# Sums of squares by one-column matmuls, taps at the front, and layer 1's memory product behind the mean matmul, in a two-layer decoder kernel

## The chip, the cores and the metric

The kernel runs on one core of a Trainium2 chip. The metric is the device time of one execution in microseconds; before the change the median of three runs is 2445.08 (2444.04 to 2449.28). TensorE is PE in the profile, VectorE DVE, ScalarE ACT, GpSimd POOL, and SP issues the DMAs.

## What is computed

A decoder trunk of two layers on x of 1024 tokens by 1024, with a memory of 256 tokens. The part that the change touches is layer 0's token mixing:

```python
mem_n = rms_norm(mem, mem_norm_g)
for l in range(DEPTH):
    mkv = (mem_n @ w_mem_kv[l]).reshape(B, MEM_LEN, 2, MEM_HEADS, HEAD_DIM)
    mk = rms_norm(mkv[:, :, 0], mem_k_norm_g[l])
    mv = mkv[:, :, 1]
    h = rms_norm(x, norm_mix_g[l])
    # layer 0
    u = h @ a_w_in[i]
    conv_out = conformer_conv(u[..., :2 * CONV_W] + a_b_glu[i], a_dw[i], a_dw_b[i], a_ln_g[i], a_ln_b[i])
    qm = rms_norm(u[..., 2 * CONV_W:].reshape(B, S, MEM_HEADS, HEAD_DIM), mem_q_norm_g[l])
    mix = jnp.concatenate([conv_out, memory_attention(qm, mk, mv)], axis=-1)
    x = x + mix @ w_out[l]
    x = x + squared_relu_mlp(rms_norm(x, norm_mlp_g[l]), w_mlp_in[l], w_mlp_out[l])
```

`conformer_conv` multiplies by a sigmoid gate, runs a causal depthwise convolution of 31 taps over 768 channels, and ends in a layer norm over the 768 channels and a silu. Layer 1 (sparse attention over shared keys and values) is not touched.

## The kernel before

Channels lie on the 128 partitions and tokens along the free axis, in two halves of 512 tokens. A tile is 128x512 in fp32. Each product is three matmuls (high x high, high x low, low x high parts, `mm3`, L80 to L82); `weight` splits a weight tile (ACT L110 the high part, POOL or DVE L111 the low part), and L87/L88 do the same for activations.

A framework with a scheduler puts each engine's instructions into one fixed order, from the order in which the code yields them and from its own model of time. On an engine nothing overtakes: an instruction that waits holds up all that stand behind it.

`layer0` runs layer 0's mixing. Its front, `load(hf)`, brings the eight x tiles of a half in (16 DMAs of 256 KB on SP for both halves) and squares them on ACT; DVE and POOL add the squares into two tiles `facc` (L559). `norm_steps` then makes the RMS norm: `col_stats` sums each column over the partitions by matmuls whose moving operand has one column of ones (L151, four for each part, result `ps_n`), DVE takes the inverse root in three Newton steps (`rsqrt`, L93 to L97) and spreads it over a diagonal (`diag`, L157), and a matmul with ones broadcasts it to all partitions (`ps_r`, L165). DVE multiplies x by it (`h`, L181).

Between the two halves' norms stands layer 0's memory product, `mem_kv`: `product` (L273 to L275, into `ps_mkv`) and `put`, which normalizes the keys by head (`hm`, `hr`, `kn`, split into `khl`) and transposes them by matmuls with the identity (`ps_dk`, L219). Layer 1's memory product is the same code, run later.

Then come six convolution tiles. For tile i of a half the input projection gives `ps_a`, ACT the gate, DVE the gated value `vA` (first half) or `vB` (second half) (L535). `conv(i)` runs 22 of the 31 taps on DVE (L495 the first, L497 the others, into `ca` in PSUM), and nine on ACT and POOL (L500 to L504, `cmore`); L506 adds both, and POOL adds the result to `csum` (L510). The letters of `ORDER` give the sequence in which the code issues these pieces (A and B a tile's projections, M and X the memory queries and attention, F and G the end of the convolution's norm, N and Z the steps of the memory product).

`conv_norm` makes the layer norm of the convolution: `ps_mu` (L634) is the sum over channels of `csum`, DVE subtracts the mean from each tile (L638), ACT squares it (`csq`), POOL and DVE add the squares (L647, L649), `col_stats` and `ps_r` follow as above, DVE scales (L656), and ACT and DVE form the silu (`z`, `t`, L661 to L664). Its eight `act` tiles (six from here and two from the memory attention) go into the output projection, `ps_wo` (L407 to L409).

The taps are loaded after `later()` has opened the pools that follow the front.

Of the kernel before, what the change touches and what calls it, by code (L numbers as in the profile page):

```python
# [89 lines left out]

def rsqrt(nc, r, m, t):

    nc.vector.tensor_scalar(r.bitcast(I32), m.bitcast(I32), -0.5, 1597463007.0, op0=ALU.mult, op1=ALU.add)  # L93
    for _ in range(3):
        nc.vector.tensor_mul(t, r, r)
# [46 lines left out]


def col_stats(k, parts, n, eps, ps=None):

    nc = k.nc
    if ps is None:
        ps = k.psum.tile([P, HF], F32, tag=k.tag, name="ps_n", bufs=k.nps)
    for i, a in enumerate(parts):
        for j in range(4):  # L150
            nc.tensor.matmul(ps[:, j:j + 1], lhsT=a[:, j * P:(j + 1) * P], rhs=k.ones[:, 0:1],  # L151
                             start=(i == 0 and j == 0), stop=(i == len(parts) - 1 and j == 3))
    m, r, t = (k.tmp.tile([P, 4], F32, tag=n_, name=n_, bufs=2) for n_ in ("nm", "nr", "nt"))
    nc.vector.tensor_scalar(m, ps[:, 0:4], 1.0 / n, eps, op0=ALU.mult, op1=ALU.add)
    rsqrt(nc, r, m, t)
    d = k.tmp.tile([P, 4, P], F32, tag="diag", name="diag", bufs=1)
    nc.vector.tensor_mul(d, k.ident[:, None, :].to_broadcast([P, 4, P]), r[:, :, None].to_broadcast([P, 4, P]))  # L157
    return d
# [80 lines left out]

def mem_kv(k, mp, zp, kv0, kv1, kvd, room):  # L240

# [23 lines left out]
    def product(l):  # L265
        pss = [k.psum.tile([P, HF], F32, tag="mm", name="ps_mkv", bufs=4) for _ in range(2)]
        for kt in range(KT):
            at = slice(kt % 2 * 512, kt % 2 * 512 + 512)
            hl = weight(k, k.i["w_mem_kv"][l, kt // 2][:, at], raw=raws[kt // 2][:, at] if l == 0 else None)
            for tt in range(2):  # L270
                ah = mh[kt][:, 0, tt * P:(tt + 1) * P]
                al = mh[kt][:, 1, tt * P:(tt + 1) * P]
                nc.tensor.matmul(pss[tt], lhsT=ah, rhs=hl[:, 0], start=(kt == 0), stop=False)  # L273
                nc.tensor.matmul(pss[tt], lhsT=ah, rhs=hl[:, 1], start=False, stop=False)
                nc.tensor.matmul(pss[tt], lhsT=al, rhs=hl[:, 0], start=False, stop=(kt == KT - 1))  # L275
        k.pe(10400)
# [208 lines left out]
def conv(k, i, v, taps, out, csum, pool, nd):  # L485
# [27 lines left out]
def layer0(k, act, later, finish, dst, kvd, m0d, room, act_b):  # L513

# [5 lines left out]
    with ExitStack() as left:  # L520
# [25 lines left out]
        with tc.tile_pool(name="xfront", bufs=1, side="right") as xp:  # L546

            def load(hf):
                x, acc = [], [xp.tile([P, HF], F32, tag="facc", name="facc", bufs=4) for _ in range(2)]
                for kt in range(KT):  # L550
                    x.append(xp.tile([P, HF], F32, tag="x", name="x", bufs=15))
                    nc.sync.dma_start(x[kt], k.i["x"][hf, :, kt])
                    if kt < 2:
                        nc.scalar.activation(acc[kt], x[kt], AF.Square)
# [4 lines left out]
                    (nc.gpsimd if j else nc.vector).tensor_tensor(acc[j], acc[j], sq, op=ALU.add)  # L559
# [69 lines left out]
def conv_norm(k, mix, cvs, csum, early, order):  # L629
# [3 lines left out]
    ps = k.psum.tile([P, HF], F32, tag=k.tag, name="ps_mu", bufs=k.nps)  # L633
    nc.tensor.matmul(ps, lhsT=k.ones, rhs=csum, start=True, stop=True)  # L634
    acc = csum
    for n, i in enumerate(order):
        c = cvs[i]
        nc.vector.scalar_tensor_tensor(c, ps, -1.0 / 768, c, op0=ALU.mult, op1=ALU.add)  # L638
        if not early:
            sq_add(k, csum, c, n == 0)  # L640
            continue
        t = csum if n == 0 else k.tmp.tile([P, HF], F32, tag="acc" if n == 3 else "a", name="csq", bufs=2)
        if n == 3:
            acc = t
        mark = nc.scalar.activation(t, c, AF.Square)
        if n not in (0, 3):
            (nc.vector if n > 3 else nc.gpsimd).tensor_tensor(acc, acc, t, op=ALU.add)  # L647
    if early:
        nc.vector.tensor_add(csum, csum, acc)  # L649
    d = col_stats(k, [csum], 768, 1e-5)  # L650
    r = col_bcast(k, d)
# [741 lines left out]
```

## Time and profile before

| what | value |
|---|---|
| median of three runs | 2445.08 us |
| lowest, highest | 2444.04, 2449.28 us |
| the profiled execution | 2451.38 us |
| its span | 2449.6 us |
| its mean granted PE clock | 0.988 |

The profile is of one execution, a little longer than the median. Its span counts from the first to the last instruction. A row of its timeline gives the start, how long the instruction lasts, its engine and line, what it writes and reads, and in brackets for how long the engine had been idle and what ended that. PE's rows overlap, since matmuls are pipelined; the distance from one start to the next is the pace.

### The profile page before, as it was taken

What the parts mean: (1) busy time and instruction counts of PE and PEld (TensorE: products, weight loads), DVE (VectorE), ACT (ScalarE), POOL (GpSimd) and SP (SyncE); (2) the same over time, 40 slices, a digit from 0 to 9 for tenths busy, and PEclk for the clock granted to TensorE, in tenths of its full rate; (3) what the DMA queues carried; (4) which work ended last, traced back from release to release, by engine and by line L of the source; (5) the groups of instructions that cost most, each with busy time, mean ns of one, the idle gap of its engine ahead of it and who ended that gap; (6) DMA issues with size and microseconds to landing.
All of it is one profiled execution on the core that took longest, in us unless ns stands there. A gap on an engine that the chain in (4) does not pass through costs nothing.

```text
span 2449.6 us, 36781 instructions
## 1 busy us (share of the span) xinstructions
PE 2362.6 (96%) x12098; PEld 1994.6 (81%) x12098; DVE 1669.2 (68%) x3590; ACT 1293.3 (53%) x2938; POOL 1229.9 (50%) x1060
## 2 busy tenths in 40 slices
PE   5998899999988999999999999999999999999999
PEld 4887687888777988888887888888888887788887
DVE  7897586998668667777436866778787765333333
ACT  5575555333545457777434545666766654333332
POOL 2876544545643256566445324565566542344443
PEclk9999999999999999999999999999999999999999
DMA  5212433323344332322335443322222226233233
GB/s 186 80 55 84 151 97 101 102 92 95 123 128 141 112 115 84 91 79 79 114 103 171 136 130 92 112 64 67 80 80 63 62 67 206 69 95 97 93 96 103
DMA packets 157214, 250.87 MB, mean 102 GB/s; under 512 B 17632, under 2 KB 48992, under 8 KB 156512
## 3 DMA queue, kind: packets, MB, share of 16 engines
q1 hardware_dynamic: 157024, 248.52, 33.0%
q8 instruction: 96, 1.57, 0.3%
q14 instruction: 94, 0.77, 0.1%
HBM read 217.52 MB, written 20.45 MB: 97 GB/s over the span
## 4 chain that ended last, share of the span: by engine, by line
PE 62%; DVE 4%; DMA 3%; issue 2%; ACT 1%; POOL 1%; SPq 0%; ACTq 0%; DVEq 0%; POOLq 0%
PE ps_i L448 7%; PE ps_i L450 7%; PE ps_i L449 7%; PE ps_mo L80 6%; PE ps_mo L82 6%; PE ps_mo L81 6%; PE ps_t L1054 4%; PE ps_s L1010 4%; PE ps_o L1070 2%; PE ps_o L1073 2%; PE ps_tok L688 1%; PE ps_tok L687 1%; PE ps_tok L689 1%; PE ps_wo L409 1%; PE ps_wo L407 1%
## 5 line engine op out<-in xcount | busy, mean ns | idle before, releaser
L111 POOL TENSOR_TENSOR hl<-raw,hl 128x512 fp32r<-128x512 f32 x596 | 778.6, 1317 | 873.8 <-ACT hl L110 830.7
L110 ACT ACTIVATE hl<-raw 128x512 fp32r<-128x512 f32 x648 | 405.1, 630 | 631.6 <-PE ps_i L450 258.1
L470 DVE TENSOR_TENSOR x<-x,ps_mo 128x512 f32<-128x512 f32 x512 | 348.3, 683 | 136.8 <-PE ps_mo L82 133.4
L80 PE MATMUL ps_mo<-hid,hl 128*128 128x512 f32 x1024 | 409.3, 400 | 6.9 <-DVE x L470 6.7
L448 PE MATMUL ps_i<-act,hl 128*128 128x512 f32 x1024 | 407.5, 398 | 8.2 <-DVE x L411 6.9
L450 PE MATMUL ps_i<-act,hl 128*128 128x512 f32 x1024 | 405.7, 396 | 0.0
L449 PE MATMUL ps_i<-act,hl 128*128 128x512 f32 x1024 | 404.0, 395 | 1.2 <-DVE act L417 1.2
L82 PE MATMUL ps_mo<-hid,hl 128*128 128x512 f32 x1024 | 401.2, 392 | 0.0
L81 PE MATMUL ps_mo<-hid,hl 128*128 128x512 f32 x1024 | 400.9, 391 | 0.0
L448 PEld LDWEIGHTS ps_i<-act,hl 128*128 128x128 f32 x1024 | 193.7, 189 | 49.4 <-DVE x L411 7.3
L80 PEld LDWEIGHTS ps_mo<-hid,hl 128*128 128x128 f32 x1024 | 192.3, 188 | 49.5 <-DVE x L470 12.7
L456 DVE SCALAR_TENSOR_TENSOR a<-ps_i,r 128x512 f32<-128x512 f32 x128 | 88.0, 689 | 206.5 <-PE ps_i L450 201.6
L449 PEld LDWEIGHTS ps_i<-act,hl 128*128 128x128 f32 x1024 | 193.6, 189 | 41.8 <-DVE act L417 2.2
L450 PEld LDWEIGHTS ps_i<-act,hl 128*128 128x128 f32 x1024 | 193.5, 189 | 41.9 <-issue 0.5
L82 PEld LDWEIGHTS ps_mo<-hid,hl 128*128 128x128 f32 x1024 | 192.2, 188 | 41.1
L81 PEld LDWEIGHTS ps_mo<-hid,hl 128*128 128x128 f32 x1024 | 192.7, 188 | 37.0 <-issue 0.5
L1021 ACT ACTIVATE prob<-ps_s,small 128x512 f32<-128x512 f32 (+3 forms) x240 | 141.1, 590 | 83.0 <-DVE small L1019 52.7
L1040 POOL TENSOR_TENSOR prob<-prob,small 128x1024 f32<-128x1024 f32 (+3 forms) x120 | 180.0, 1524 | 1.3 <-DVE small L1034 0.8
L1062 DVE TENSOR_TENSOR PT<-ps_t,PT 128x512 fp32r<-128x512 f32 (+1 forms) x220 | 147.0, 671 | 48.2 <-ACT PT L1058 46.9
L1058 ACT ACTIVATE PT<-ps_t 128x512 fp32r<-128x512 f32 (+1 forms) x256 | 142.3, 566 | 60.9 <-PE ps_t L1054 55.0
L1010 PE MATMUL ps_s<-KS,Q 128*128 128x512 f32 (+5 forms) x552 | 143.1, 358 | 0.0
L88 DVE TENSOR_TENSOR hid<-a,hid 128x512 fp32r<-128x512 f32 x128 | 100.6, 787 | 59.0 <-ACT hid L87 58.3
(295 smaller groups left out, 4708.8 us busy)
## 6 DMA issues: line engine op xcount, KB each, us to landing
raw<-in_w_mlp_in_dram SPq DMA_DIRECT2D x256, 256.0 KB, 2.8
raw<-in_w_mlp_out_dram SPq DMA_DIRECT2D x256, 256.0 KB, 2.9
raw<-in_w_out_dram SPq DMA_DIRECT2D x64, 256.0 KB, 3.3
Q<-Q SPq DMA_DIRECT2D x160, 64.0 KB, 2.0
raw<-in_cmp_w_dram SPq DMA_DIRECT2D x32, 256.0 KB, 2.7
raw<-in_a_w_dram SPq DMA_DIRECT2D x24, 256.0 KB, 3.0
raw<-in_b_wq_dram SPq DMA_DIRECT2D x24, 256.0 KB, 2.7
mixd<-ev SPq DMA_DIRECT2D x80, 64.0 KB, 2.1
```

Source lines behind the costliest of these rows:

```text
L80: nc.tensor.matmul(ps, lhsT=lh, rhs=rh, start=(i == 0), stop=False)
L81: nc.tensor.matmul(ps, lhsT=lh, rhs=rl, start=False, stop=False)
L82: nc.tensor.matmul(ps, lhsT=ll, rhs=rh, start=False, stop=(i == n - 1))
L110: nc.scalar.activation(hl[:, 0, :n], raw[:, :n], AF.Copy)
L111: k.last_lo = k.lo_eng.tensor_tensor(hl[:, 1, :n], raw[:, :n], hl[:, 0, :n].bitcast(F32), op=ALU.subtract)
L448: nc.tensor.matmul(p_, lhsT=wh, rhs=h[kt][:, 0], start=kt == 0, stop=False)
L449: nc.tensor.matmul(p_, lhsT=wh, rhs=h[kt][:, 1], start=False, stop=False)
L450: nc.tensor.matmul(p_, lhsT=wl, rhs=h[kt][:, 0], start=False, stop=kt == KT - 1)
L470: nc.vector.tensor_add(x[o], x[o], ps)
L1010: nc.tensor.matmul(o_, lhsT=lhs, rhs=rhs, start=(n_ == 0), stop=(n_ == len(mms) - 1))
L1040: nc.gpsimd.tensor_tensor(t, t, sc[:, :, None].to_broadcast([P, 2, t.shape[-1]]), op=ALU.mult)
L1062: nc.vector.tensor_sub(PT[:, 1, :m], Tv[:, :m], PT[:, 0, :m].bitcast(F32))
```

## The change

1. `col_sums`: the one-column matmuls take the squares tile by tile. At the front each x tile's square goes straight into four of them (32 for a half, 8 before); the adds into `facc` go, and four square tiles `fsq` are kept in place of two. In the first half's conv norm (`early`) the six squares give 24 matmuls where four stood; the adds L647 and L649 go. The second half's conv norm keeps its adds.
2. The last convolution tile is no longer added to `csum`; a second matmul adds it into `ps_mu`.
3. `rsqrt` multiplies in another order, and in `col_stats` the values m, t and the last r stand in columns of `ps_n`'s PSUM bank.
4. The taps are loaded behind the first half's x tiles, into a pool that lives through the kernel.
5. Layer 1's memory product is issued after the mean matmul, and its `put` comes behind the last step of the conv norm (`Z1` at the end of `ORDER`).

```diff
-ORDER = "B0A1M0X0B1A2A3B2A4B3A5B4B5F0M1Z0G0N1"
+ORDER = "B0A1M0X0B1A2A3B2A4B3A5B4B5F0M1Z0G0N1Z1"
...
-    for _ in range(3):
-        nc.vector.tensor_mul(t, r, r)
-        nc.vector.scalar_tensor_tensor(t, t, -0.5, m, op0=ALU.mult, op1=ALU.mult)
-        nc.vector.scalar_tensor_tensor(r, t, 1.5, r, op0=ALU.add, op1=ALU.mult)
+    for i in range(3):
+        nc.vector.tensor_mul(t, r, m)
+        nc.vector.scalar_tensor_tensor(t, t, -0.5, r, op0=ALU.mult, op1=ALU.mult)
+        nc.vector.scalar_tensor_tensor(r if last is None or i < 2 else last, t, 1.5, r, op0=ALU.add, op1=ALU.mult)
...
+def col_sums(k, ps, a, first, last):
+    for j in range(4):
+        k.nc.tensor.matmul(ps[:, j:j + 1], lhsT=a[:, j * P:(j + 1) * P], rhs=k.ones[:, 0:1], start=(first and j == 0),
+                           stop=(last and j == 3))
...
-    m, r, t = (k.tmp.tile([P, 4], F32, tag=n_, name=n_, bufs=2) for n_ in ("nm", "nr", "nt"))
+    r = k.tmp.tile([P, 4], F32, tag="nr", name="nr", bufs=2)
+    m, t, last = (ps[:, 4 * i:4 * i + 4] for i in range(1, 4))
...
+                if l == 1:
+                    es.enter_context(k.tc.issue_after(behind().ins))
...
     pss = product(1)
+    yield
     KS, V = kv1()
...
-    else:
+    elif i < 5:
         nc.gpsimd.tensor_tensor(csum, csum, out, op=ALU.add)
...
-                    if kt < 2:
-                        nc.scalar.activation(acc[kt], x[kt], AF.Square)
-                        continue
-                    sq = xp.tile([P, HF], F32, tag="fsq", name="fsq", bufs=2)
+                    sq = xp.tile([P, HF], F32, tag="fsq", name="fsq", bufs=4)
                     nc.scalar.activation(sq, x[kt], AF.Square)
-                    j = 1 if kt in (3, 6) else 0
-                    (nc.gpsimd if j else nc.vector).tensor_tensor(acc[j], acc[j], sq, op=ALU.add)
+                    col_sums(k, ps, sq, kt == 0, kt == KT - 1)
...
             na = load(0)
+            nc.sync.dma_start(taps, k.i["taps"].rearrange("p (i l) -> p i l", i=6))
...
-    nc.tensor.matmul(ps, lhsT=k.ones, rhs=csum, start=True, stop=True)
-    acc = csum
+    nc.tensor.matmul(ps, lhsT=k.ones, rhs=csum, start=True, stop=False)
+    k.mean = nc.tensor.matmul(ps, lhsT=k.ones, rhs=cvs[5], start=False, stop=True)
...
-        if n not in (0, 3):
-            (nc.vector if n > 3 else nc.gpsimd).tensor_tensor(acc, acc, t, op=ALU.add)
-    if early:
-        nc.vector.tensor_add(csum, csum, acc)
-    d = col_stats(k, [csum], 768, 1e-5)
+        col_sums(k, pq, t, n == 0, n == 5)
+    d = col_stats(k, [], 768, 1e-5, pq) if early else col_stats(k, [csum], 768, 1e-5)
```

The lines move by this: L151 becomes L148, L157 L166, L165 L174, L154 L163, L93 to L97 L94 to L98, L181 L190, L219 L228, L495 and L497 L510 and L512, L535 L550, L273 to L275 L287 to L289, L407 L422, L656 L665, L664 L673, L712 L721.

The scheduler's order changes at three places. The first is DVE at the end of the front's second norm. Before, the inverse root (L154 to L157, on `ps_n`) follows the gated value of the first tile, with operations of the head norm (`kn`) between:

```order
L535 SCALAR_TENSOR_TENSOR vA<-ps_a,glu 128x512
L154 TENSOR_SCALAR nm<-ps_n 128x4
L88 TENSOR_TENSOR khl<-kn,khl 128x4x64
L93 TENSOR_SCALAR nr<-nm 128x4
L201 TENSOR_TENSOR kn<-kv,hr 128x256
L95 TENSOR_TENSOR nt<-nr 128x4
L202 TENSOR_TENSOR kn<-kn,rows 128x256
L96 SCALAR_TENSOR_TENSOR nt<-nt,nm 128x4
L97 SCALAR_TENSOR_TENSOR nr<-nt,nr 128x4
L95 TENSOR_TENSOR nt<-nr 128x4
L96 SCALAR_TENSOR_TENSOR nt<-nt,nm 128x4
L97 SCALAR_TENSOR_TENSOR nr<-nt,nr 128x4
```

Of the change, from the same `vA` on:

```order
L550 SCALAR_TENSOR_TENSOR vA<-ps_a,glu 128x512
L510 TENSOR_SCALAR ca<-vA,taps,cols 128x512
L512 SCALAR_TENSOR_TENSOR ca<-vA,taps,ca 128x512 x8
L163 TENSOR_SCALAR ps_n<-ps_n 128x4
L512 SCALAR_TENSOR_TENSOR ca<-vA,taps,ca 128x512
L94 TENSOR_SCALAR nr<-ps_n 128x4
L512 SCALAR_TENSOR_TENSOR ca<-vA,taps,ca 128x512
L96 TENSOR_TENSOR ps_n<-nr,ps_n 128x4
L512 SCALAR_TENSOR_TENSOR ca<-vA,taps,ca 128x512
L97 SCALAR_TENSOR_TENSOR ps_n<-ps_n,nr 128x4
L512 SCALAR_TENSOR_TENSOR ca<-vA,taps,ca 128x512
L98 SCALAR_TENSOR_TENSOR nr<-ps_n,nr 128x4
```

The first tile's convolution (L510, L512 into `ca`), which stood behind the eight `h` before, now stands ahead of the inverse root and between its steps; it goes on so to `diag`, with eleven L512 in all from L163 to L166, and two more behind that.

The second place is PE there. Before:

```order
L82 MATMUL ps_a<-act_97,hl 128x512
L151 MATMUL ps_n<-ones,facc 128x1 x4
L165 MATMUL ps_r<-diag,ones 128x512
L219 MATMUL ps_dk<-ident,khl 128x128 x4
L80 MATMUL ps_a<-act_345,hl 128x512 x2
```

Of the change:

```order
L81 MATMUL ps_a<-act_98,hl 128x512
L82 MATMUL ps_a<-act_98,hl 128x512
L148 MATMUL ps_n<-ones,fsq 128x1 x28
L174 MATMUL ps_r<-diag,ones 128x512
L228 MATMUL ps_dk<-ident,khl 128x128 x4
L80 MATMUL ps_a<-act_363,hl 128x512 x2
```

The 28 sums of seven squares stand together behind the last `ps_a` matmul, where four stood (the other four, and the four of the first square now, stand among the matmuls before).

The third is PE around the layer 1 memory product. Before, the mean matmul `ps_mu` stands in the product; at the product's end, the sums (`csum`), the transposes of its two token tiles (`ps_dk`), the broadcast and the output projection:

```order
L274 MATMUL ps_mkv<-hl,mh 128x512
L275 MATMUL ps_mkv<-hl,mh 128x512
L151 MATMUL ps_n<-ones,csum_611 128x1 x4
L219 MATMUL ps_dk<-ident,khl 128x128 x4
L165 MATMUL ps_r<-diag,ones 128x512
L219 MATMUL ps_dk<-ident,khl 128x128 x4
L407 MATMUL ps_wo<-act_90,hl 128x512 x2
```

Of the change, where the sums stand in the product, and its end:

```order
L289 MATMUL ps_mkv<-hl,mh 128x512
L288 MATMUL ps_mkv<-hl,mh 128x512
L148 MATMUL ps_n<-ones,csum_645 128x1 x4
L148 MATMUL ps_n<-ones,csq 128x1 x20
L289 MATMUL ps_mkv<-hl,mh 128x512
L287 MATMUL ps_mkv<-hl,mh 128x512
...
L288 MATMUL ps_mkv<-hl,mh 128x512
L289 MATMUL ps_mkv<-hl,mh 128x512
L174 MATMUL ps_r<-diag,ones 128x512
L228 MATMUL ps_dk<-ident,khl 128x128 x8
L422 MATMUL ps_wo<-act_91,hl 128x512
```

The broadcast stands right behind the product, and both groups of transposes stand between it and the output projection. The two mean matmuls stand ahead of the product, the second one six matmuls ahead. On DVE the steps of the conv norm's inverse root now stand together, ahead of the operations of the head norm, and those stand among the scalings and silu steps of the convolution.

More of the change, by code (lines that the diff above doesn't have):

```diff
@@ L149, in col_stats @@
     for i, a in enumerate(parts):
-        for j in range(4):
-            nc.tensor.matmul(ps[:, j:j + 1], lhsT=a[:, j * P:(j + 1) * P], rhs=k.ones[:, 0:1],
-                             start=(i == 0 and j == 0), stop=(i == len(parts) - 1 and j == 3))
-    m, r, t = (k.tmp.tile([P, 4], F32, tag=n_, name=n_, bufs=2) for n_ in ("nm", "nr", "nt"))
+        col_sums(k, ps, a, i == 0, i == len(parts) - 1)
+    r = k.tmp.tile([P, 4], F32, tag="nr", name="nr", bufs=2)
+    m, t, last = (ps[:, 4 * i:4 * i + 4] for i in range(1, 4))
     nc.vector.tensor_scalar(m, ps[:, 0:4], 1.0 / n, eps, op0=ALU.mult, op1=ALU.add)
-    rsqrt(nc, r, m, t)
+    rsqrt(nc, r, m, t, last)
     d = k.tmp.tile([P, 4, P], F32, tag="diag", name="diag", bufs=1)
-    nc.vector.tensor_mul(d, k.ident[:, None, :].to_broadcast([P, 4, P]), r[:, :, None].to_broadcast([P, 4, P]))
+    nc.vector.tensor_mul(d, k.ident[:, None, :].to_broadcast([P, 4, P]), last[:, :, None].to_broadcast([P, 4, P]))
     return d
@@ L235, in query_stack, with mem_kv @@
     return Q
-def mem_kv(k, mp, zp, kv0, kv1, kvd, room):
+def mem_kv(k, mp, zp, kv0, kv1, kvd, room, behind):
     nc = k.nc
@@ L269, in product @@
             hl = weight(k, k.i["w_mem_kv"][l, kt // 2][:, at], raw=raws[kt // 2][:, at] if l == 0 else None)
[L270 to L275, printed above, removed]
+            with ExitStack() as es:
+                if l == 1:
+                    es.enter_context(k.tc.issue_after(behind().ins))
+                for tt in range(2):
+                    ah = mh[kt][:, 0, tt * P:(tt + 1) * P]
+                    al = mh[kt][:, 1, tt * P:(tt + 1) * P]
+                    nc.tensor.matmul(pss[tt], lhsT=ah, rhs=hl[:, 0], start=(kt == 0), stop=False)
+                    nc.tensor.matmul(pss[tt], lhsT=ah, rhs=hl[:, 1], start=False, stop=False)
+                    nc.tensor.matmul(pss[tt], lhsT=al, rhs=hl[:, 0], start=False, stop=(kt == KT - 1))
         k.pe(10400)
@@ L508, in conv, with layer0 @@
         nc.gpsimd.tensor_copy(csum, out)
-    else:
+    elif i < 5:
         nc.gpsimd.tensor_tensor(csum, csum, out, op=ALU.add)
-def layer0(k, act, later, finish, dst, kvd, m0d, room, act_b):
+def layer0(k, act, later, finish, dst, kvd, m0d, room, act_b, taps):
     nc, tc = k.nc, k.tc
@@ L548, in load @@
             def load(hf):
-                x, acc = [], [xp.tile([P, HF], F32, tag="facc", name="facc", bufs=4) for _ in range(2)]
+                x, ps = [], k.psum.tile([P, HF], F32, tag=k.tag, name="ps_n", bufs=k.nps)
                 for kt in range(KT):
@@ L579, in layer0 @@
             k.flush()
-        vB, cvs, csum, taps = later()
+        vB, cvs, csum = later()
         pr = left.enter_context(tc.tile_pool(name="pair", bufs=1, side="right"))
-        nc.sync.dma_start(taps, k.i["taps"].rearrange("p (i l) -> p i l", i=6))
         def taps_of(i, vA):
@@ L592, in layer0 @@
                 last = finish(cvs, csum)
-                next(last)
+                mean = next(last)
             elif what == "G":
@@ L1218, in finish_conv @@
             next(steps)
-            yield
+            yield kl.mean
             if hf == 0:
@@ L1227, in build @@
         layer0(k, act, later, lambda *a: finish_conv(0, *a), mem_dst(mixd, 0), kvd, m0d,
-               lambda i: pslot[1](4 + i, [P, 2 * HF], F32, "mkvw"), lambda: act_tiles(1))
-        vB, cvs, csum, taps = kept
+               lambda i: pslot[1](4 + i, [P, 2 * HF], F32, "mkvw"), lambda: act_tiles(1), taps)
+        vB, cvs, csum = kept
         late = pool(es, "late")
```

18 lines of the change are left out of this document (9 added, 9 removed).

## The prediction

> **What bounds the kernel now.** The page comes first.
>
> ```profile
> span 2449.6 us, 36781 instructions
> PE 2362.6 (96%) x12098; PEld 1994.6 (81%) x12098; DVE 1669.2 (68%) x3590; ACT 1293.3 (53%) x2938; POOL 1229.9 (50%) x1060
> ```
>
> PE is busy for 96%, so time can be won or lost only where PE waits. Second, PE's waits in the first 450 us (columns: group that waits, what it waited for, us in total, times, longest):
>
> ```profile
> PE ps_n L151 <- DVE facc L559: 13.7, 1, 13.7
> PE ps_r L165 <- DVE diag L157: 12.3, 3, 6.7
> PE ps_n L151 <- DVE csum L649: 7.0, 1, 7.0
> PE ps_wo L407 <- ACT act L87: 4.5, 1, 4.5
> PE ps_dk L219 <- DVE khl L88: 3.2, 1, 3.2
> PE ps_wo L407 <- DVE hm L712: 1.3, 1, 1.3
> ```
>
> These are the three norms that the change touches: x of the front's two halves (ps_n, ps_r), and the conv norm. Third, busy time by stage (x counts instructions; then granted PE clock, DMA share, GB/s):
>
> ```profile
> core 0: us, PE busy (x) PEld busy (x) DVE busy (x) ACT busy (x) POOL busy (x), PEclk, DMA share, GB/s
> 50.00:70.00 20.00, 12.64 (x39) 9.16 (x40) 16.09 (x49) 6.53 (x12) 3.87 (x3) 0.66 0.06 26
> 70.00:110.00 40.00, 40.00 (x222) 34.68 (x221) 35.41 (x52) 25.89 (x43) 36.97 (x33) 1.00 0.34 109
> ...
> 150.00:190.00 40.00, 40.00 (x201) 33.55 (x200) 37.41 (x70) 31.47 (x75) 25.24 (x22) 1.00 0.18 49
> 190.00:218.00 28.00, 28.00 (x175) 24.91 (x174) 25.08 (x40) 13.93 (x30) 17.93 (x15) 1.00 0.22 65
> ...
> 231.00:256.00 25.00, 9.61 (x29) 6.50 (x28) 21.05 (x57) 12.68 (x25) 8.08 (x7) 0.61 0.29 95
> ```
>
> From 70 to 218 PE is busy without a gap at a clock of 1.00, and DVE is not (35.41 of 40). So what the front loses before 70 isn't caught up before 218; the holes are 50 to 70 and 231 to 256.
>
> **Part A, the first half's norm.** Rows of the timeline from here on: start, us, engine, line, operation, out<-in, shapes, count, and in brackets the idle time before and what ended it.
>
> ```profile
> 4.67 1.32 ACT L554 ACTIVATE facc<-x 128x512 f32<-128x512 f32 x2 [2.65 <-DMA x<-in_x_dram]
> ...
> 13.73 3.54 PE L151 MATMUL ps_n<-ones,facc 128*128 128x1 f32 x16 [13.73 <-DVE facc L559]
> ...
> 22.24 2.07 PE L165 MATMUL ps_r<-diag,ones 128*128 128x512 f32 x2 [4.96 <-DVE diag L157]
> ...
> 49.05 0.94 PE L151 MATMUL ps_n<-ones,facc 128*128 128x1 f32 x8
> 56.70 2.08 PE L165 MATMUL ps_r<-diag,ones 128*128 128x512 f32 x2 [6.70 <-DVE diag L157]
> ```
>
> A one-column matmul leaves two records: 3.54/8 = 0.44 us cold, 0.94/4 = 0.235 warm. 32 in place of 8 take 14.1 us cold, spread over the arriving x tiles; from the end of the first square, 4.67 + 0.7 = 5.4, they are done at 19.5 if the clock stays cold, by 16 if it warms, in place of 13.73 + 3.54 = 17.3. Between 17.3 and diag the same weight splits stand on DVE as before, and cover part of it. I carry **+0.7** (0 to 1.4) into all that follows.
>
> **Part B, the second half's norm.** Now the sums are 28 one-column matmuls behind the last ps_a matmul, 28 x 0.235 = 6.6 us, from 49.05 + 0.7 = 49.8 to 56.4. That alone would cost little: before, diag ended at 56.65. The DVE order decides. It has vA, the first lag L510 and eight L512 ahead of the rsqrt, then an L512 ahead of each of its steps.
>
> ```profile
> 49.89 0.65 ACT L533 ACTIVATE ps_a<-ps_a,halves 128x512 f32<-128x512 f32 x1
> ...
> 52.06 0.42 DVE L202 TENSOR_TENSOR kn<-kn,rows 128x256 f32<-128x256 f32 x1
> ...
> 52.47 0.68 DVE L535 SCALAR_TENSOR_TENSOR vA<-ps_a,glu 128x512 f32<-128x512 f32 x1
> 53.07 0.15 DVE L154 TENSOR_SCALAR nm<-ps_n 128x4 f32<-128x4 f32 x1
> ...
> 55.96 0.69 DVE L157 TENSOR_TENSOR diag<-ident,nr 128x512 f32<-128x512 f32 x1
> ...
> 73.11 0.81 DVE L495 TENSOR_SCALAR ca<-vA,taps,cols 128x512 f32<-128x512 f32 x1 [2.19 <-DMA taps<-in_taps_dram]
> 73.96 6.29 DVE L497 SCALAR_TENSOR_TENSOR ca<-vA,taps,ca 128x512 f32<-128x512 f32 x8
> ```
>
> The lags wait for taps before (2.19 us at 73.11); now taps land early, and the lags may run. vA ends at 51.2 if only ps_a holds it (49.8 + 0.65 + 0.7), at 54.8 if the head norm is as late as before, now with its second kn and khl ahead of vA (52.5, khl 0.4, kn 0.85, vA 0.65, and waits). I take 53, as the head norm loses some of the facc adds ahead of it. Then L510 0.85, eight L512 6.29, L163 0.2, and eleven pairs of an L512 and a small operation. The price of a pair:
>
> ```profile
> 99.22 0.75 DVE L497 SCALAR_TENSOR_TENSOR ca<-vA,taps,ca 128x512 f32<-128x512 f32 x1
> 99.88 0.28 DVE L698 TENSOR_SCALAR hm<-hm 128x16 f32<-128x16 f32 x1
> 100.08 0.74 DVE L497 SCALAR_TENSOR_TENSOR ca<-vA,taps,ca 128x512 f32<-128x512 f32 x1
> ...
> 101.34 0.74 DVE L497 SCALAR_TENSOR_TENSOR ca<-vA,taps,ca 128x512 f32<-128x512 f32 x1
> 102.00 0.68 DVE L95 TENSOR_TENSOR ht<-hr 128x16 f32<-128x16 f32 x1
> ```
>
> From 99.22 to 100.08 a pair takes 0.86; from 100.08 to 101.34, with a small operation in SBUF, 1.26. The new steps have m, t and the last r in PSUM, like nm's 0.15 at 53.07, so I take 0.86: 9.5 us (13.9 by the dear pair). The Trainium skill, "SBUF — State Buffer", section "Who interferes with whom", says that only the port pair shared by VectorE and GpSimd contends; the two prices agree with it, and it would leave the PSUM steps at the cheap one. Then diag 0.69. Sum: 53 + 0.85 + 6.29 + 0.2 + 9.5 + 0.7 = 70.5 for a ps_r that began at 56.70: **+13.8 us** (12.0 from vA at 51.2, 15.6 from 54.8; A is in it). The conv lags that now stand ahead would have been done beside PE anyway, so nothing comes back: conv 5 needs vB5, which PE sets.
>
> **Part C, the mean matmul.** Two passes of 1.02/2 are added and two that stood inside the memory product (224.19) now stand before it; ps_tok ends where PE has done them all: **+0.9** at the start P of the memory product (219.86 before).
>
> ```profile
> 219.86 0.39 PE L273 MATMUL ps_mkv<-hl,mh 128*128 128x512 f32 x1
> 220.09 0.40 PE L274 MATMUL ps_mkv<-hl,mh 128*128 128x512 f32 x1
> ...
> 224.19 1.02 PE L634 MATMUL ps_mu<-csum,ones 128*128 128x512 f32 x2
> ...
> 238.84 1.87 PE L151 MATMUL ps_n<-ones,csum 128*128 128x1 f32 x8 [7.01 <-DVE csum L649]
> ...
> 245.66 2.08 PE L165 MATMUL ps_r<-diag,ones 128*128 128x512 f32 x2 [0.60 <-DVE diag L157]
> ...
> 253.14 1.22 PE L407 MATMUL ps_wo<-act,hl 128*128 128x512 f32 x2 [4.54 <-ACT act L87]
> ...
> 254.58 0.63 PE L409 MATMUL ps_wo<-act,hl 128*128 128x512 f32 x1
> 255.01 0.63 PE L408 MATMUL ps_wo<-act,hl 128*128 128x512 f32 x1
> ...
> 247.78 4.04 DVE L656 SCALAR_TENSOR_TENSOR conv<-ps_r,halves,conv 128x512 f32<-128x512 f32 x6 [1.31 <-PE ps_r L165]
> ```
>
> **Part D, the conv norm and w_out.** Before, w_out begins at P + 33.3. Now: 23 of 48 product matmuls, 23 x 0.23 (219.86 to 220.09) = 5.2; 24 sums x 0.235 = 5.6, at P + 10.9; rsqrt and diag (11 x 0.2 + 0.7) hide behind the other 25 matmuls, which end at P + 16.6; ps_r 1.0 warm, R = P + 17.7. So the waits of 7.0 and 0.6 go. But PE's order now has **both ps_dk groups ahead of w_out**, and each needs the head norm of put(1) (khl), which starts only when the product ends. On DVE there stand, between R and the second khl: the six conv scalings 4.0; ten operations on 128x256 (V, hm, kn, khl) at 0.41, as from 52.06 to 52.47, 4.1; six t, three act splits and one hm at 0.6, as from 52.47 to 53.07, 6.0; the head norm's 24 small steps at 0.1 to 0.2, 2.4 to 4.8. That is 16.5 to 18.9 of work; ACT's 12 z and t (0.65 each, like ps_a at 49.89) run beside it, but DVE waits for some of them, and I take 19. With ps_dk, w_out starts near R + 19.8 = P + 37.5: **+4.2** (+1.7 with the least work and no wait; +9 if each small step takes 0.4). The stall of 1.3 behind w_out goes, **-1.3**, and w_out starts cold longer, **+0.4**.
>
> A rule speaks against the N=1 sums. In the row of 231 to 256 the granted clock is 0.61 after a gap of 7 us. The Trainium skill, "TensorE: Matmul & The Clock Gate", Part 1, says that an idle window of about 3.4 us returns TensorE to half clock; the trace agrees in kind, and whether one-column matmuls count as busy no run here shows.
>
> Outside the first 300 us the instructions keep their order, and nothing is charged there.
>
> **The sum.** 13.8 + 0.9 + 4.2 - 1.3 + 0.4 = +18.0 us. The profiled execution took 2451.38 (span 2449.6, 1.8 around it), 6.3 above the median of 2445.08. Against its own time that is 2469.4; the same 18.0 on the median give **2463.1**. By the bounds, the least is 12.0 + 0.9 + 1.7 - 1.3 = +13.3 (2458.4), the most 15.6 + 0.9 + 9 - 1.3 + 0.8 = +25.0 (2470.1), and the dear pair in B would add 13.9 - 9.5 = 4.4 to any of them.
>
> **Rivals.**
> 1. *Same.* put(1) doesn't hold w_out: its khl comes early, beside the conv scaling. For it: nm took 0.15, so small steps alone don't fill 19 us. Then w_out follows ps_r as before by 7.5 (245.66 to 253.14), at P + 24.1, 9.2 earlier, and with B at its least the sum is 12.0 + 0.9 - 9.2 - 1.3 + 0.4 = +2.8: 2447.9. Against it: the order. Chance 0.10. That the layer 1 product doesn't come behind the mean matmul is no case of its own: the order shows that it does.
> 2. *Faster.* DVE, not PE, is the bound from 73 to 253. Then lags run ahead are no loss, since DVE has to run them anyway, and what counts is what DVE sheds: the chain to csum, for which PE waits 7.0, and the wait for taps, 2.2: -9.2, 2435.9. It decides from the point at which DVE has no idle time left there; its 35.41 and 37.41 of 40 against PE's 40.00 speak against it. Chance 0.07.
> 3. *Slower still.* One-column matmuls don't hold the clock. Then the 25 product matmuls and the ps_r behind them run at about 0.43 a piece (a cold w_out pair starts 254.58 to 255.01 in the trace), 25 x 0.2 = +5: 2468.1, or 2472.5 with the dear pair in B. For it: such a gap did leave the clock at 0.61. Against it: the sums stand between matmuls of 512 columns. Chance 0.13.
>
> **How the numbers follow.** Forecast 0.70; the rivals 0.10, 0.07, 0.13. 0.2%, 4.9 us, is about what a measurement of this kernel can tell from no change. Slower by more: 0.70 + 0.13 = 0.83; within: 0.10; faster: 0.07. The forecast's own range is 2458 to 2470. The range for the whole takes in the first rival and most of the third: 2447 to 2472, which leaves out rival 2 and the far ends.
>
> **What would show it.** A: ps_r within 1.5 us of 22.2. B: L163 of the second half behind eight L512, and ps_r near 70.5, with a PE gap of about 14 us ahead of it. C: two mean passes just before the product. D: no PE gap between product and ps_r, then one of about 19 us before w_out, put down to khl. It is wrong if ps_r comes before 65, if PE has gaps between 85 and 230, or if ps_dk doesn't end the wait of w_out.

## The result and the profile after

| | us |
|---|---|
| changed kernel, median of 4 runs | 2479.95 (2478.18 to 2481.99) |
| kernel before beside it, 4 runs | 2447.18 (2444.04 to 2450.78) |
| ratio, 95% interval | 1.013, 1.0112 to 1.0147 |
| the profiled execution of the changed kernel | 2479.01, granted clock 0.985 |

The change makes the kernel 32.8 us slower. The direction was forecast, but the time lies 7.95 us above the top of the range. The two traces differ by 2479.01 - 2451.38 = 27.6 us only, since the profiled execution of before was 6.3 us above its median; what follows takes places from the traces and sizes from the timed runs.

The page of the changed kernel, first lines:

```profile
span 2477.2 us, 37042 instructions
PE 2394.4 (97%) x12238; PEld 2014.7 (81%) x12238; DVE 1651.1 (67%) x3579; ACT 1295.9 (52%) x2938; POOL 1214.5 (49%) x1052
```

PE is busy for 2394.4 - 2362.6 = 31.8 us more, and idle for 2477.2 - 2394.4 = 82.8 us where it was 2449.6 - 2362.6 = 87.0. So the loss isn't new waiting in sum: PE has more to do, or does it more slowly. Its waits in the first 480 us of the changed kernel (group that waits, what for, us in total, times, longest):

```profile
PE ps_dk L228 <- DVE khl L88: 18.2, 2, 14.8
PE ps_r L174 <- DVE diag L166: 14.1, 2, 11.0
PE ps_n L148 <- ACT fsq L569: 6.4, 2, 5.5
```

The waits for `facc` and `csum` are gone, and one of 18.2 us for the keys of layer 1 has come. The timeline of PE in the changed kernel at the three places (start, us, engine, line, operation, out<-in, shapes, count, idle before and its end):

```profile
5.51 13.78 PE L148 MATMUL ps_n<-ones,fsq 128*128 128x1 f32 x64 [5.51 <-ACT fsq L569]
22.40 2.07 PE L174 MATMUL ps_r<-diag,ones 128*128 128x512 f32 x2 [3.10 <-DVE diag L166]
...
53.35 3.58 PE L148 MATMUL ps_n<-ones,fsq 128*128 128x1 f32 x16 [0.92 <-ACT fsq L569]
67.89 2.08 PE L174 MATMUL ps_r<-diag,ones 128*128 128x512 f32 x2 [10.96 <-DVE diag L166]
...
232.45 1.02 PE L646 MATMUL ps_mu<-conv,ones 128*128 128x512 f32 x2
234.01 0.40 PE L287 MATMUL ps_mkv<-hl,mh 128*128 128x512 f32 x1
...
239.25 0.95 PE L148 MATMUL ps_n<-ones,csum 128*128 128x1 f32 x8
240.06 5.18 PE L148 MATMUL ps_n<-ones,csq 128*128 128x1 f32 x40
245.10 0.77 PE L289 MATMUL ps_mkv<-hl,mh 128*128 128x512 f32 x1
245.68 0.63 PE L287 MATMUL ps_mkv<-hl,mh 128*128 128x512 f32 x1
246.10 0.63 PE L288 MATMUL ps_mkv<-hl,mh 128*128 128x512 f32 x1
...
250.78 0.40 PE L287 MATMUL ps_mkv<-hl,mh 128*128 128x512 f32 x1
...
253.52 1.02 PE L174 MATMUL ps_r<-diag,ones 128*128 128x512 f32 x2
269.38 1.12 PE L228 MATMUL ps_dk<-ident,khl 128*128 128x128 f32 x4 [14.83 <-DVE khl L88]
273.89 1.12 PE L228 MATMUL ps_dk<-ident,khl 128*128 128x128 f32 x4 [3.40 <-DVE khl L88]
274.66 0.78 PE L422 MATMUL ps_wo<-act,hl 128*128 128x512 f32 x1
```

The second half's broadcast comes at 67.89 for 56.70, 11.2 later; the memory product at 234.01 for 219.86, 14.15 later; the output projection at 274.66 for 253.14, 21.5 later, and 20.2 once before's later stall is taken off. A stretch is new here: behind the 24 one-column sums, 13 product matmuls go at (250.78 - 245.10)/13 = 0.44 us a piece, the other 12 at (253.52 - 250.78)/12 = 0.23. (Matmuls at the slower of these two paces are called cold below.) The windows there (busy time of the engines, granted clock, DMA share, GB/s):

```profile
core 0: us, PE busy (x) PEld busy (x) DVE busy (x) ACT busy (x) POOL busy (x), PEclk, DMA share, GB/s
239.00:245.00 6.00, 6.00 (x50) 5.93 (x48) 0.00 (x0) 0.35 (x1) 1.90 (x2) 0.91 0.37 116
245.00:251.00 6.00, 6.00 (x16) 4.73 (x16) 2.52 (x12) 1.26 (x2) 2.56 (x2) 0.52 0.12 44
251.00:254.00 3.00, 3.00 (x14) 2.25 (x12) 0.00 (x0) 2.21 (x4) 2.18 (x2) 1.00 0.27 87
```

PE has no gap in these 15 us, and yet the granted clock falls to 0.52.

That leaves more than the first 300 us can hold. A third of the MLP's input products (`ps_i`, their first line) as the groups of lines show them (duration in ns least/median/most, first and last start), before and after:

```profile
L448 PE MATMUL ps_i<-act,hl x1024: 387/394/796, 301.2 to 2423.2; 128*128 128x512 f32 x171
```

```profile
L463 PE MATMUL ps_i<-act,hl x1024: 387/394/798, 321.1 to 2450.9; 128*128 128x512 f32 x171
```

The first starts 19.9 us later, the last 27.7 us later: 7.8 us come where neither an instruction nor its order was changed. Within a run of these matmuls the difference grows steadily: at matched instructions it is 20.6 at 421 us, 21.1 at 483, 21.6 at 534. Between such runs it moves both ways (22.6 at 778, 21.3 at 882), and it ends at 27.5 at 2400. PE is idle for 1999.60 - 1957.65 = 42.0 us beyond 450 us before, and for 41.1 beyond 480 after, so it isn't waiting. What is left is the pace. One group of 48 `ps_i` matmuls that nothing interrupts, its first and last row, before:

```profile
439.26 0.40 PE L448 MATMUL ps_i<-act,hl 128*128 128x512 f32 x1
...
450.04 0.39 PE L450 MATMUL ps_i<-act,hl 128*128 128x512 f32 x1
```

and after:

```profile
460.02 0.39 PE L463 MATMUL ps_i<-act,hl 128*128 128x512 f32 x1
...
470.99 0.39 PE L465 MATMUL ps_i<-act,hl 128*128 128x512 f32 x1
```

The same 47 steps take 10.97 us for 10.78, that is 0.2334 a step for 0.2294. Over the 3072 `ps_i` matmuls 0.0040 would be 12 us (10.8 by the means of all of their steps, 0.2333 and 0.2298); summed over their starts the two traces differ by 7.8. The products `ps_wo` and `ps_a`, which like `ps_i` stream an `act` tile, slow down too (0.2306 to 0.2333, 0.2311 to 0.2332); `ps_mo`, which streams `hid`, does not (0.2288, 0.2287).

### The profile page after: what moved, and what is told of

It reads as the page before. It is cut to its first block, busy times and chain, and to the rows that moved or that the text cites. A ratio compares the mean times of both kernels' runs of the same rounds, so it can differ in the third digit from the quotient of the medians.

```text
span 2477.2 us, 37042 instructions
## 1 busy us (share of the span) xinstructions
PE 2394.4 (97%) x12238; PEld 2014.7 (81%) x12238; DVE 1651.1 (67%) x3579; ACT 1295.9 (52%) x2938; POOL 1214.5 (49%) x1052
## 4 chain that ended last, share of the span: by engine, by line
PE 62%; DVE 4%; DMA 3%; issue 2%; POOL 1%; ACT 1%; SPq 0%; ACTq 0%; POOLq 0%; DVEq 0%
PE ps_i L463 7%; PE ps_i L465 7%; PE ps_i L464 7%; PE ps_mo L80 6%; PE ps_mo L82 6%; PE ps_mo L81 6%; PE ps_t L1063 4%; PE ps_s L1019 4%; PE ps_o L1079 2%; PE ps_o L1082 2%; PE ps_tok L696 1%; PE ps_tok L698 1%; PE ps_tok L697 1%; PE ps_wo L422 1%; PE ps_wo L424 1%
```

## The experiments

Each kernel was timed beside the kernel before on the same chip. That kernel's median was 2446.89 us beside both kernels with 128 bytes in the pool, the one with the taps as before and the one without layer 1's head norm; 2447.4 beside those with 64 and 192 bytes, the conv norm alone and the product ahead of the last conv tiles; and 2447.88 beside the rest. "Slower" and "faster" by so many us are differences from these medians; differences from the changed kernel are from its 2479.95.

**Is it the place of the tiles?** The change moves every tile behind the constants, since the taps now lie there, and m and t have left a pool between the weights' tiles and `act`. So `act` lies 128 bytes nearer to the weights. The theory: where the tiles lie in SBUF sets the pace. The rival: something in the changed order does. A tile that no one reads, in that pool, moves `act` and leaves the order alone.

```diff
         k.rpool = k.tmp
+        spare = k.tmp.tile([P, 32], F32, name="spare")
+        nc.gpsimd.memset(spare, 0.0)
```

The kernel before with it:

> The kernel before with one unused 128-byte tile ahead of the act tiles; every engine's order is the same as before. The trace of after shows that from 300 us on, matmuls that read act tiles (ps_i, ps_a, ps_wo) follow each other every 0.2333 us, where before it was 0.2293, while those that read hid (ps_mo) keep 0.228. Theory P (place): the start address of the act tiles sets that pace; before it was 128 bytes above a multiple of 256, after on a multiple of 256, and here it is on a multiple of 256 too. P expects ps_i at 0.233 and +6 to +8 us over the kernel before, spread evenly over the time. Rival (the pace differs from run to run or from chip to chip): ps_i at 0.229 or like the kernel before on the same chip, 0 us.

2458.98 us, ratio 1.0054 (1.0037 to 1.0072): 12.1 us slower, by a tile that does nothing. The group of 48 takes 10.97 us, as in the changed kernel. The pace was as expected; the size was above it.

The changed kernel with the same tile:

> The changed kernel with the same unused 128-byte tile; orders as in after. The act tiles then start 128 bytes above a multiple of 256, as before. Theory P expects ps_i at 0.229 and -6 to -8 us against after (about 2472), with the first 300 us less than 2 us changed. Rival: no change against after, 2480.

2469.85 us, ratio 1.0093 (1.0073 to 1.0112): 10.1 us less than the changed kernel, and the group takes 10.78 as before. So about 10 of the 32.8 us are the tiles' place.

Other sizes in the kernel before, 64 bytes (`[P, 16]`) and 192 (`[P, 48]`):

> The kernel before with an unused 64-byte tile, orders as before: the act tiles start 192 bytes above a multiple of 256. If only a multiple of 256 is slow, ps_i keeps 0.230 and the time 2447. If the place counts within 128 bytes, as between the weights (64 above) and the act tiles, ps_i changes; the hid tiles lie 64 above and run at 0.2287, so 0.2285 and -2 us are the other outcome.

2458.42 us, ratio 1.0044 (1.0028 to 1.006); group 10.96. Neither of the two outcomes that were named came: the pace is the slow one.

> The kernel before with an unused 192-byte tile, orders as before: the act tiles start 64 bytes above a multiple of 256, as the hid tiles and the weights do. If the place relative to 256 alone sets the pace, ps_i runs like ps_mo, 0.2287, and the time falls by 2 to 4 us; if only a multiple of 256 is slow, nothing changes.

2439.21 us, ratio 0.9961 (0.9948 to 0.9974): 8.2 us faster than before, where 2 to 4 were expected, with the same instructions in the same order but for the spare tile's memset. Its group:

```profile
436.83 0.39 PE L448 MATMUL ps_i<-act,hl 128*128 128x512 f32 x1
...
447.48 0.39 PE L450 MATMUL ps_i<-act,hl 128*128 128x512 f32 x1
```

10.65 us. Is it the address of `act` itself, or its distance from the weights? 128 bytes among the constants move both together, `act` to the address that it has in the slow kernel with 128 bytes in the pool (0 beyond a multiple of 256):

```diff
         k.mqg = cp.tile([P, 3, 64], F32, name="qg")
+        spare = cp.tile([P, 32], F32, name="spare")
+        nc.gpsimd.memset(spare, 0.0)
```

> The kernel before with an unused 128-byte tile ahead of the weights, so that the weights' hl tiles, hid and act all move by 128 bytes and keep their distances; orders as before. Modulo 256 bytes the act tiles then start at 0, the weights and hid at 192. Theory R (the distance of the moving tile from the weights sets the pace: 0 bytes 0.228, 64 bytes 0.230, 128 bytes 0.233, 192 bytes 0.233): ps_i 0.230, ps_mo 0.229, the time as before. Theory S (the moving tile's own address does): ps_i 0.233 as on a multiple of 256, ps_mo 0.233 as at 192, and +20 us or more over before.

2447.47 us, ratio 0.9998 (0.9987 to 1.0009), group 10.78 as before, where `act` at the same address with the weights unmoved had 10.97: the address of `act` isn't what counts. In the programs' layout, the first `act` tile lies this far behind the first weight tile, beyond a multiple of 256 bytes:

| kernel | distance beyond a multiple of 256 B | 48 `ps_i` matmuls, us |
|---|---|---|
| before + 192 B; the last kernel below | 0 | 10.65 |
| before; after + 128 B; before with all moved by 128 B | 64 | 10.78 |
| before + 64 B | 128 | 10.96 |
| changed kernel; before + 128 B | 192 | 10.97 |

`hid` lies at 0 in all of them, and `ps_mo` hardly changes (0.2283 to 0.2289). The kernels that follow fit the table too. From the first `ps_i` matmul to the last, the six traces with 64 take 2119.9 us in the mean (2115.6 to 2124.4), and the six with 128 or 192 take 2129.4 (2124.7 to 2136.1). That is 9.5 us more; the trace of before, with 2122.5, is one of the longer ones at 64, so that it and the changed kernel's showed only 7.8. What in SBUF or in PE makes it so, no run shows.

**The front: sums or lags?** The lags are the steps of the convolution on DVE, one for each tap. The changed kernel with the taps' tile and load where they were, so that the lags can't run ahead, and all else of the change kept:

```diff
-        taps = cp.tile([P, 6, 31], F32, name="taps")
...
-            nc.sync.dma_start(taps, k.i["taps"].rearrange("p (i l) -> p i l", i=6))
...
+            kept.append(rp.tile([P, 6, 31], F32, name="taps"))
```

> The changed kernel with the taps tile and its load back where they were. The order of DVE then has the second norm's rsqrt and diag straight behind vA, with no L512 between. Theory B (the lags ahead of the rsqrt cost the front 11 us): ps_r of the second half starts near 60 in place of 67.9, since the sums end at 57, and the time falls by 8 (about 2472). The act tiles lie on a multiple of 256 here too, so theory P expects the slow pace of 0.233 to stay; if the 744 bytes of taps alone mattered, it would go and the time fall by 15. Rival to B (the front's delay is caught up later): no change.

2470.82 us, ratio 1.0092 (1.0074 to 1.011): 9.1 us less than the changed kernel. PE in its front, and the window:

```profile
48.97 9.48 PE L148 MATMUL ps_n<-ones,fsq 128*128 128x1 f32 x56
61.45 2.07 PE L174 MATMUL ps_r<-diag,ones 128*128 128x512 f32 x2 [2.99 <-DVE diag L166]
```

```profile
core 0: us, PE busy (x) PEld busy (x) DVE busy (x) ACT busy (x) POOL busy (x), PEclk, DMA share, GB/s
48.00:56.00 8.00, 8.00 (x51) 7.78 (x49) 3.25 (x13) 2.77 (x5) 0.00 (x0) 0.73 0.03 12
```

The broadcast comes at 61.45, a little later than expected. Of the 11.2 us, 67.89 - 61.45 = 6.4 are the lags, and 61.45 - 56.70 = 4.75 the sums. By the first `ps_i` matmul the trace is 7.5 us ahead of the changed kernel's (313.53 for 321.08); the timed runs say 9.1. The 28 sums took 9.48 us and not 28 x 0.235 = 6.6: with PE busy for 8.00 of 8.00 us the clock fell to a mean of 0.73. The group of 48 takes 10.97, so the taps' own bytes are not what slowed it.

The other way round, the taps' tile alone, in the kernel before:

```diff
+        ctaps = cp.tile([P, 6, 31], F32, name="taps")
...
-            kept.append(rp.tile([P, 6, 31], F32, name="taps"))
+            kept.append(ctaps)
```

> The kernel before with nothing changed but the pool of the taps tile: it lies in the pool that lives through the kernel, and its load stands where it stood. Act tiles and weights move by 768 bytes together, so no theory of place expects anything. DVE's order then has the first lag and ten others of the first tile between the steps of the second norm's rsqrt, with two kn among them, but no eight ahead of it. Theory B: ps_r of the second half starts 8 to 9 us later than before (near 65), and the time is +8 (2455). Rival (the lags only matter when the sums are late): +2 or less.

2454.57 us, ratio 1.0031 (1.0019 to 1.0044): 6.7 us slower. The load stands where it stood; that the tile no longer waits for a pool of its own is enough for the lags to be put ahead. Its broadcast waits for the diagonal for 17.52 us:

```profile
66.35 2.08 PE L165 MATMUL ps_r<-diag,ones 128*128 128x512 f32 x2 [17.52 <-DVE diag L157]
```

There the steps of the inverse root lie in SBUF, and POOL begins at 53.43 (DVE and POOL of this kernel, two pieces):

```profile
53.02 0.16 DVE L93 TENSOR_SCALAR nr<-nm 128x4 int32<-128x4 int32 x1
...
57.46 0.74 DVE L497 SCALAR_TENSOR_TENSOR ca<-vA,taps,ca 128x512 f32<-128x512 f32 x1
58.12 0.76 DVE L95 TENSOR_TENSOR nt<-nr 128x4 f32<-128x4 f32 x1
58.80 0.74 DVE L497 SCALAR_TENSOR_TENSOR ca<-vA,taps,ca 128x512 f32<-128x512 f32 x1
...
64.83 0.15 DVE L97 SCALAR_TENSOR_TENSOR nr<-nt,nr 128x4 f32<-128x4 f32 x1
```

```profile
53.43 10.80 POOL L504 TENSOR_TENSOR cmore<-cmore,cprod 128x512 f32<-128x512 f32 x8 [8.83 <-ACT cprod L503]
```

A step of four columns takes 0.16 before POOL begins, 0.76 beside it, 0.15 when it is done (53.43 + 10.80 = 64.23); a pair takes 58.80 - 57.46 = 1.34. In the changed kernel the steps lie in PSUM, and POOL runs from 52.86 to 63.57 too:

```profile
58.57 0.76 DVE L512 SCALAR_TENSOR_TENSOR ca<-vA,taps,ca 128x512 f32<-128x512 f32 x1
59.23 0.15 DVE L94 TENSOR_SCALAR nr<-ps_n 128x4 int32<-128x4 int32 x1
59.36 0.76 DVE L512 SCALAR_TENSOR_TENSOR ca<-vA,taps,ca 128x512 f32<-128x512 f32 x1
```

A pair takes 59.36 - 58.57 = 0.79. So part 3 of the change is a gain where it meets POOL. The Trainium skill, "SBUF — State Buffer", section "Who interferes with whom", puts the contention between VectorE and GpSimd on the SBUF ports that they share; these rows agree.

**The wait for layer 1's keys.** The changed kernel without that head norm and its transposes:

```diff
-    KS, V = kv1()
+    KS, V = kv0
     for tt in range(2):
-        put(1, tt, pss[tt], KS, V)
+        spare = zp.tile([P, HF], F32, tag="kv", name="kv", bufs=2)
+        nc.scalar.activation(spare, pss[tt], AF.Copy, scale=rm[:, tt:tt + 1])
```

> The changed kernel without layer 1's key and value normalisation behind its memory product; layer 0's keys and values go out in their place, so layer 1's memory attention is computed on those. Theory D (the transposes that stand ahead of w_out wait for the head norm): the gaps of 14.8 and 3.4 us go, w_out starts some 8 us behind ps_r as before (near 261 in place of 274.7), and the time falls by 12 to 14 (about 2467). Rival (w_out is bound by the silu and the scalings): w_out no earlier than 270, 4 us or less.

This kernel leaves that work out altogether, so it shows what waits for the work, and not what another place for it would give.

2465.67 us, ratio 1.008 (1.0056 to 1.0103): 14.3 us less than the changed kernel. PE there:

```profile
253.80 1.02 PE L174 MATMUL ps_r<-diag,ones 128*128 128x512 f32 x2
260.30 1.22 PE L423 MATMUL ps_wo<-act,hl 128*128 128x512 f32 x2 [5.48 <-ACT act L87]
```

The output projection follows the broadcast by 6.5 us, where it was 274.66 - 253.52 = 21.1. So `put` held it, as forecast.

Next, the conv norm's part of the change alone: the front's sums on DVE and POOL and the taps as before, and 128 bytes of spare tile, so that the place is that of before.

> The changed kernel with the front's sums on DVE and POOL and the taps as before, and a 128-byte tile that puts the act tiles 128 bytes above a multiple of 256 again: of the change there is left the conv norm with its sums on PE, the order of the layer 1 product, the mean in two matmuls and the rsqrt in PSUM. If front, place and conv norm are the three parts of the loss, this gives the last alone: w_out near 262 against 253.14 before, and +6 to +9 us over before (about 2454). Rival (the three parts overlap, or a fourth is hidden in the rest of the change): within 2 us of before, or more than +12.

2452.3 us, ratio 1.0016 (1.0007 to 1.0026): +4.9, a little less than expected. The wait is still the longest one of PE's list:

```profile
PE ps_dk L228 <- DVE khl L88: 18.2, 2, 14.8
```

And the same with the product and its `put` ahead of the last conv tiles, in place of behind the mean matmul:

```diff
-ORDER = "B0A1M0X0B1A2A3B2A4B3A5B4B5F0M1Z0G0N1Z1"
+ORDER = "B0A1M0X0B1A2A3B2A4B3A5Z0B4Z1B5F0M1G0N1"
...
-                if l == 1:
-                    es.enter_context(k.tc.issue_after(behind().ins))
```

> As the kernel with the conv norm alone, but layer 1's memory product is issued ahead of the projection B4 and its normalisation ahead of B5, so that nothing of it is left behind the conv norm; in PE's order the broadcast ps_r then stands among the ps_tok matmuls, and w_out behind them. Theory D expects PE to wait some 3 us for the mean and 5 us for the squares, none for khl, and w_out at once behind ps_tok: near 246 to 250, 4 to 7 us ahead of before, and about 2442. Rival (the product was needed to cover the norm, so that the waits come back as large as before): w_out at 253 or later, 2447 or more.

2444.34 us, ratio 0.9986 (0.9976 to 0.9996): 8.0 us less than with the late product, and 3.1 less than before. So the conv norm's part of the change is a gain if `put` has been done by then. The kernel before with its product moved ahead in this way, and its adds kept, was not run; so how much of the 3.1 is the one-column sums' and how much the earlier product's is not shown.

**One column or 64.** The changed kernel with sums whose moving operand has 64 columns of ones:

```diff
-        k.nc.tensor.matmul(ps[:, j:j + 1], lhsT=a[:, j * P:(j + 1) * P], rhs=k.ones[:, 0:1], start=(first and j == 0),
+        k.nc.tensor.matmul(ps[:, 64 * j:64 * j + 64], lhsT=a[:, j * P:(j + 1) * P], rhs=k.ones[:, 0:64], start=(first and j == 0),
...
```

> The changed kernel with 64 columns of ones in place of one in the sums. After the 24 sums of the conv norm the trace of after shows the product's matmuls at 0.43 a piece for 5.6 us and a granted clock of 0.52: if that is because one-column matmuls don't keep the array busy enough for the clock, 64 columns halve it or better: fewer than 6 product matmuls at 0.43 behind the sums, and from the mean matmul to ps_r some 2 us less. If the waits between them or the weight loads do it, the cold stretch stays as long. Each sum stays near 0.235 us if the weight load sets its time.

2476.09 us of two runs, ratio 1.0111 (1.0085 to 1.0137), which doesn't tell it from the changed kernel's 1.013; the trace does. PE behind the conv norm's sums, and its window:

```profile
238.10 4.63 PE L148 MATMUL ps_n<-ones,csq 128*128 128x64 f32 x40
242.54 0.48 PE L289 MATMUL ps_mkv<-hl,mh 128*128 128x512 f32 x1
242.86 0.39 PE L287 MATMUL ps_mkv<-hl,mh 128*128 128x512 f32 x1
```

```profile
core 0: us, PE busy (x) PEld busy (x) DVE busy (x) ACT busy (x) POOL busy (x), PEclk, DMA share, GB/s
242.00:248.00 6.00, 6.00 (x31) 5.06 (x31) 2.52 (x12) 2.05 (x4) 3.88 (x3) 1.00 0.19 64
```

The clock stays at 1.00 and the product matmuls behind are not cold. From the mean matmul to the broadcast it takes 248.35 - 230.46 = 17.9 us, in the changed kernel 253.52 - 232.45 = 21.1. But the same sums don't end a cold stretch. At the front of this kernel 32 of them stand in a train without a gap, and take 0.43 a piece to its end, as with one column; 20 of them take 0.23 a piece behind the warm `ps_a` matmuls:

```profile
4.83 13.88 PE L148 MATMUL ps_n<-ones,fsq 128*128 128x64 f32 x64 [4.83 <-ACT fsq L569]
...
48.06 4.57 PE L148 MATMUL ps_n<-ones,fsq 128*128 128x64 f32 x40
```

**A kernel that beats both.** The kernel with the product ahead of the last conv tiles (`Z0B4Z1B5`), its spare tile at 64 bytes in place of 128, so that the distance is a multiple of 256:

> The kernel with the product ahead of B4, with a 64-byte tile in place of the 128-byte one, so that act, hid and weights start at the same place modulo 256: the gains of the two (-3.1 and -8.2 against before) add up, ps_i at 0.228 and a time of 2436. If they don't add: 2439 or more.

2436.7 us, ratio 0.9952 (0.9938 to 0.9966): 11.2 us faster than before, about the sum of its two parts (3.1 and 8.2).

## Why the prediction was right and wrong

**The step that failed** is the sentence "Outside the first 300 us the instructions keep their order, and nothing is charged there." The order was indeed kept, but a move of 128 bytes between two pools changed the pace of the matmuls that stream `act`, and that costs 10.1 us by the timed runs. Undone by a tile of 128 bytes, the change costs 2469.85 - 2446.89 = 23.0 us, ratio 1.0073 to 1.0112, and the forecast's 18.0 on 2445.08, a ratio of 1.0074, is just inside. The prediction took the pace of 0.23 from rows of before and had no term for the layout. The diff shows which tiles move, but no row of before gives a price for that.

**The first 300 us** came out near the forecast, in part by luck. At the first `ps_i` matmul the changed kernel is 19.9 us late, where the sum has 18.0: 11.2 to the front's second broadcast (13.8 forecast), 3.0 from there to the memory product (0.9), 7.4 from there to the output projection (4.2), and -1.6 behind it (-0.9). So errors of -2.6, +2.1, +3.2 and -0.7 cancel down to +2.

**Undone one at a time**, three parts take from the changed kernel: the place 10.1, the lags 9.1, layer 1's head norm 14.3. That their sum of 33.5 is near the 32.8 lost proves little. The kernel without the head norm leaves work out, where doing it earlier gave 8.0; and the sum holds neither what the front's sums cost nor what the lost waits for `facc` and `csum` gave back. The kernel with lags, front's sums, place and late product all undone measured 3.1 us below before.

**Part A** held: the first broadcast at 22.40 for 22.24, +0.2 where +0.7 was carried; the sums stayed cold to 19.3, as the dearer end said.

**Part B** was right in its mechanism and 2.6 us too dear: the broadcast at 67.89, not 70.5. `vA` ended at 51.4, not 53, so near the least end (51.2), and a pair took 0.79, not 0.86. The choice of the cheap pair was right, but the rows that it was read from don't show why. The small operation of the pair at 0.86 (`hm`, L698) lies in SBUF like that of the pair at 1.26:

```profile
100.73 0.69 DVE L93 TENSOR_SCALAR hr<-hm 128x16 int32<-128x16 int32 x1
```

And when `nm` took 0.15, at 53.07, POOL did nothing, from 45.8 on; steps in SBUF took 0.16 beside it. That PSUM makes the difference beside a busy POOL is shown only by the kernel with the taps alone, against the changed one. That DVE decides, and not the sums, is right for the changed kernel, but the sums were no 6.6 us: with the lags gone they set the end and took 9.48.

**Part C** was too small, by a mean matmul. From the broadcast to the memory product it takes 234.01 - 67.89 = 166.1 us for 219.86 - 56.70 = 163.2. Two mean matmuls stand there now and none before. The second one, with six `ps_tok` matmuls at 0.12 behind it, takes 234.01 - 232.45 - 0.72 = 0.84, so that both are 1.7. The prediction charged only the one that is new; the one that moved ahead of the product it took out of the product's time in part D and added nowhere. Of the rest, 1.1 is the slow pace: 528 `ps_a` matmuls take 126.6 for 125.5.

**Part D** was mis-sized: +7.4 (274.66 - 234.01 = 40.65 for 253.14 - 219.86 = 33.28) where +4.2 stood, inside its bounds of 1.7 to 9. From the broadcast to the output projection the forecast had 37.5 - 16.6 = 20.9, and 21.1 were measured: the work counted on DVE was right. The error is in the product's end, P + 16.6 by forecast and P + 19.5 in the trace: 13 cold matmuls. The stall behind the output projection went, as said (-1.3), but the +0.4 for a longer cold start is not to be seen: from the output projection to the first `ps_i` matmul it takes 321.08 - 274.66 = 46.4 for 301.18 - 253.14 = 48.0.

**The rivals.** Rival 3's mechanism, that one-column matmuls don't hold the clock, is shown by the window at 0.52, the 9.48 us without a gap, and the 64 columns that mend it at the conv norm. It came beside the forecast, not in its place, and at 13 cold matmuls it cost some 2.7 us and not 5. Rival 1 fell: `put` did hold the output projection. What it would have given is seen where `put` is left out: the projection 14.36 us earlier. Rival 2 fell: with the lags back in their old place DVE has the same work, and the kernel is 9.1 us faster; so lags run ahead of the norm are a loss.

## What to carry to other kernels

When a change costs more than its places show, compare the start-to-start pace of one uninterrupted group of matmuls far from the change; if it differs, move the streamed tiles by 64 bytes at a time against the weights before the change is judged. A tile that gets a pool of longer life can let the scheduler put what reads it earlier, also ahead of what PE waits for. Sums on PE can pay where PE would wait for the adds, as at the conv norm here, but only if nothing that waits for another engine's long chain stands between them and the next product.

## What the runs showed of the hardware

- Matmuls of 512 fp32 columns run at 10.65, 10.78, 10.96 or 10.97 us per 47 steps, as the moving tile lies 0, 64, 128 or 192 bytes beyond a multiple of 256 from the weights: 3%, some 20 us of this kernel (2439.21 to 2458.98, with the same instructions in the same order but for a memset). The cause is open.
- A train of one-column matmuls without a gap lowers the granted clock (0.73 in the mean of 8 us, 0.52 in the 6 us behind 24 of them); with 64 columns the clock stayed at 1.00 in the window behind them. From a cold start 32 sums of 64 columns, 13.88 us without a gap, stayed at 0.43 a piece: they held a granted clock and did not bring it back. The Trainium skill, "TensorE: Matmul & The Clock Gate", Part 1, ties the fall to idle windows. By these rows one-column matmuls, though busy in the profile, would have to count as idle there, or nearly so.
- An operation of four columns on DVE took up to 0.76 us with its operands in SBUF beside a POOL that adds, and 0.15 to 0.16 with at least one of them in PSUM, or with POOL not running.
